# One more pair of gate strips by seven products, and fewer products beside each attention block

## The chip, the cores and the metric

The kernel runs on one core of one Trainium2 chip. The metric is the device time of one execution in microseconds (us); the number that stands for a kernel is the median of its runs. Five engines work side by side: TensorE (PE in the profile) multiplies matrices, VectorE (DVE) and ScalarE (ACT) do element-wise work, GpSimd (POOL) does little here, and SyncE (SP) issues most of the DMAs.

## The reference

One decoder layer on 1024 tokens of width 1024: a SwiGLU half step, a mixer with three branches (an RWKV-7 recurrence, sliding-window attention, cross-attention into 256 memory tokens), and a second SwiGLU half step. What the change touches is the projection into the mixer and the gates that merge the branches:

```python
p_rwkv, p_swa, q_mem, gate_logits = _split(u @ w_in[l], IN_SIZES)
...
g_a, g_b, g_c = _split(jax.nn.sigmoid(gate_logits + gate_b[l]), (D, D, D))
merged = (g_a * (y_a @ w_branch[l, 0]) + g_b * (y_b @ w_branch[l, 1])
          + g_c * (y_c @ w_branch[l, 2]))
```

The gates are 3072 columns of w_in, that is 24 strips of 128 columns, gates 0 to 23.

## The kernel before

**Products.** Everything runs feature-major: a strip of 128 weight columns is multiplied with all 1024 tokens, in two halves of 512. A float32 block is split into a high and a low part (ScalarE casts the high part, line 300, VectorE subtracts it, line 302), and each block product is three matmuls of 128 x 128 on 512 columns (lines 377 to 379). In what follows a *product* is one such matmul; the lumps below are counted in them.

**Two ways to do a strip.** The plain way (`gate_block`, line 1457; in the profile its sums are `pgate`) takes 8 blocks x 2 halves x 3 = 48 products for a strip, 96 for two. The paired way (`win_pair`, line 1407; sums `px`, `py`, `pz`) takes two strips and two halves as a 2 x 2 block matrix and does it with seven half-size products instead of eight: 7 x 4 x 3 = 84. It needs sums of weights, which `operands` (lines 327 to 333) has VectorE make, sums of the inputs (`mix_form`, made once for all pairs), and more steps that put the seven results together (lines 1426 and 1433). Before the change seven pairs are done that way: three of attention strips and gates 2 to 9. The list is `WIN_PAIRS`, line 56.

**The stages of the mixer, in the order of TensorE's stream.** Preparation of the recurrence; two plain gates; the pairs; beside pairs 4 and 5 the corner of a triangular inverse (sums `corner`, small matmuls); the last pair, beside which the first chunks of the recurrence are fetched; the chain of the recurrence (`rwkv_chain`, 16 chunks, each a series of small dependent matmuls `z`, `y`, `gram`, `bkt`), with the plain gates `GATES_FIRST` to `GATES_EARLY` - 1 in its gaps (line 1795); the end of the recurrence; and attention.

**What is beside attention.** `filling` (line 1471) is one long series of products without a place of its own: the plain gates from `GATES_EARLY` to 23, then the first two branch projections (sums `pb`). `fill(n, ...)` takes the next n of them. `attention` (line 1658) has 8 memory blocks and then 8 window blocks. Each block does its scores (`msc` or `sc`), its softmax on VectorE and ScalarE, its transposes (`mptr` or `ptr`) and its values (`mpv` or `pv`), and between these it takes a lump from the series: 42 and 32 products at the first two blocks, then `LUMPS[0]` = 29 at each memory block and `LUMPS[1]` = 52 at each window block. What is left of the series is done behind the last block. Scores, transposes and values share four PSUM banks; a block of window scores needs all four.

**Sums in passing.** `unit` (line 683) is called once behind each plain gate from the start of attention and once behind each strip of the branch projections. Each call makes one of eleven sets of weight sums for the second feed-forward: four VectorE steps (lines 668 to 671) on tiles that SyncE has loaded, and four stores. A set holds two of the four `wide` buffers (line 660; named `gin` in the profile). The other user of these four buffers is the branch projection, which loads a stored gate into one (line 1719, issued by ScalarE's queue), multiplies it with the branch (line 1728) and so frees it.

**What sets the order.** The program is written for a scheduler, which fixes one order for each engine; each engine then works its list from front to end.

Of the kernel before, what the change touches and what calls it, by code (L numbers as in the profile page):

```python
# [47 lines left out]
ATT_BLOCKS = (18, 19, 14, 15, 16, 17, 20, 21, 22, 23)  # L48
GATES_PLAIN = 2
CORNER = (4, 4)  # L50
GATES_FIRST = 10
GATES_EARLY = 12
LUMPS = (29, 52)
MIX_SUMS = ("t2", "t1", "t3", "t4")
PARTS = 5
WIN_PAIRS = ((16, 17), (20, 21), (22, 23)) + tuple((24 + g, 25 + g) for g in range(GATES_PLAIN, GATES_FIRST, 2))

# [174 lines left out]
class Builder:  # L232
# [13 lines left out]
    def plan(self):  # L246
        io, seq = self.io, []
        for f in ("ffn1", "ffn2"):
# [3 lines left out]
            if f == "ffn1":  # L252
# [6 lines left out]
                seq += [("win_pair", i) for i in range(len(WIN_PAIRS))]  # L259
                seq += [("win", 24 + g) for g in range(GATES_FIRST, 24)]  # L260
                seq += [("wb", 4 * i + q) for i in BRANCHES + BRANCHES[2:] for q in range(4)]
# [1209 lines left out]
    def filling(self, u, pool, gate_d, y_d):  # L1471

        for g in range(GATES_EARLY, 22):
            ps = {h: self.psum("pgate") for h in (0, 1)}
# [266 lines left out]
    def mixer(self, u, cp, close_raws, att_d, gate_d, km_d, vm_d):  # L1741
# [22 lines left out]
        with tc.tile_pool(reuse_waits="tile", name="gates", bufs=2) as gp:  # L1764
# [27 lines left out]
            with chunks, tc.tile_pool(reuse_waits="tile", name="chain", bufs=2) as pool:  # L1792
                y = pool.tile([P, NPAIR, T], F32, name="y", bufs=1)
                last = self.rwkv_chain(pool, early, fetched, pk_d, inv_d, y)
                for g in range(GATES_FIRST, GATES_EARLY):
                    self.gate_block(g, u, gp, gate_d)
# [5 lines left out]
            with tc.tile_pool(reuse_waits="tile", name="att", bufs=1) as ap, tc.tile_pool(name="attw", bufs=2) as pool:  # L1802
# [53 lines left out]
                blocks += [WindowBlock(self, pool, b, att_d=att_d, sws=sws, tables=(cos, sin), kd=kd, vt=vt, vd=vd, y_d=y_d[1]) for b in range(nb)]  # L1856
                self.attention(blocks, [42, 32] + [LUMPS[0]] * (nb - 2) + [LUMPS[1]] * nb, {0: [tables], 1: [keys], 2: [load_values], 4: [turn_values]})
                for _ in self.fills:
# [209 lines left out]
```

## Time and profile before

| | us |
|---|---|
| runs of the kernel before, median of 3 | 2256.55 |
| lowest, highest | 2255.4, 2257.11 |
| the profiled execution, its own time | 2257.27 |
| its span, first to last instruction | 2255.6 |
| TensorE busy in it | 2227.7 |
| VectorE busy | 1642.0 |
| ScalarE busy | 1028.9 |

The profiled execution is 0.72 us over the median and its time is 1.67 us more than its span. A busy matmul engine is not one at its peak, since matmuls are pipelined and overlap in the record; how long one takes in a stream is read from the starts of consecutive ones.

### The profile page before, as it was taken

What the parts mean: (1) busy time and instruction counts of PE and PEld (TensorE: products, weight loads), DVE (VectorE), ACT (ScalarE), POOL (GpSimd) and SP (SyncE); (2) the same over time, 40 slices, a digit from 0 to 9 for tenths busy, and PEclk for the clock granted to TensorE, in tenths of its full rate; (3) what the DMA queues carried; (4) which work ended last, traced back from release to release, by engine and by line L of the source; (5) the groups of instructions that cost most, each with busy time, mean ns of one, the idle gap of its engine ahead of it and who ended that gap; (6) DMA issues with size and microseconds to landing.
All of it is one profiled execution on the core that took longest, in us unless ns stands there. A gap on an engine that the chain in (4) does not pass through costs nothing.

```text
span 2255.6 us, 34511 instructions
## 1 busy us (share of the span) xinstructions
PE 2227.7 (99%) x12304; PEld 1832.2 (81%) x12304; DVE 1642.0 (73%) x2761; ACT 1028.9 (46%) x1933; POOL 58.8 (3%) x114
## 2 busy tenths in 40 slices
PE   8999999999999999999999999999999999999998
PEld 6888888888887788877878887788888888888887
DVE  6988767766698887863667577794898886656576
ACT  6523333454556654444355454444663223345451
POOL 0000000000000000000330000000000000000000
PEclk9999999999999999999999999999999999999999
DMA  8565666686665356464538877564565552347663
GB/s 292 174 202 169 202 210 214 229 294 205 191 210 188 120 150 204 155 169 153 158 95 276 270 252 250 185 202 142 174 214 176 194 189 100 114 164 249 205 196 121
DMA packets 279132, 431.90 MB, mean 191 GB/s; under 512 B 58512, under 2 KB 96912, under 8 KB 278704
## 3 DMA queue, kind: packets, MB, share of 16 engines
q1 hardware_dynamic: 266160, 409.96, 56.0%
q10 hardware_dynamic: 12800, 19.73, 2.7%
q8 instruction: 97, 1.59, 0.3%
q14 instruction: 75, 0.61, 0.1%
HBM read 292.75 MB, written 135.79 MB: 190 GB/s over the span
## 4 chain that ended last, share of the span: by engine, by line
PE 51%; DMA 1%; DVE 1%; ACT 1%; issue 0%; SPq 0%; DVEq 0%; ACTq 0%
PE px L377 4%; PE px L379 4%; PE px L378 4%; PE po L377 3%; PE po L378 3%; PE po L379 3%; PE pgate L377 2%; PE pgate L378 2%; PE pgate L379 2%; PE pz L377 2%; PE pz L379 2%; PE pz L378 2%; PE pb L377 2%; PE pb L378 2%; PE pb L379 2%; PE pw L378 1%
## 5 line engine op out<-in xcount | busy, mean ns | idle before, releaser
L300 ACT CAST w_hi<-w_raw 128x512 fp32r<-128x512 f32 x608 | 376.2, 620 | 725.0 <-PE px L378 189.9
L302 DVE TENSOR_TENSOR w_lo<-w_raw,w_hi 128x512 fp32r<-128x512 f32 x608 | 417.3, 688 | 191.0 <-ACT w_hi L300 171.7
L379 PE MATMUL po<-u,w_lo 128*128 128x512 f32 (+1 forms) x476 | 180.9, 380 | 0.0
L378 PE MATMUL po<-u,w_hi 128*128 128x512 f32 (+1 forms) x476 | 180.9, 380 | 0.0
L377 PE MATMUL po<-u,w_hi 128*128 128x512 f32 (+1 forms) x476 | 180.9, 380 | 0.0
L377 PE MATMUL px<-u,w_hi 128*128 128x512 f32 x380 | 147.9, 389 | 0.8 <-DVE km L1596 0.8
L377 PE MATMUL pz<-u,w_hi 128*128 128x512 f32 x380 | 148.1, 390 | 0.0
L378 PE MATMUL px<-u,w_hi 128*128 128x512 f32 x380 | 147.9, 389 | 0.0
L379 PE MATMUL px<-u,w_lo 128*128 128x512 f32 x380 | 147.8, 389 | 0.0
L379 PE MATMUL pz<-u,w_lo 128*128 128x512 f32 x380 | 147.8, 389 | 0.0
L378 PE MATMUL pz<-u,w_hi 128*128 128x512 f32 x380 | 147.8, 389 | 0.0
L377 PE MATMUL px<-f,w_hi 128*128 128x512 f32 x352 | 137.1, 390 | 0.0
L379 PE MATMUL px<-f,w_lo 128*128 128x512 f32 x352 | 137.0, 389 | 0.0
L378 PE MATMUL px<-f,w_hi 128*128 128x512 f32 x352 | 136.9, 389 | 0.0
L486 DVE TENSOR_TENSOR u<-hid,u 128x512 fp32r<-128x512 f32 x114 | 78.3, 690 | 44.7 <-ACT u L485 43.7
L378 PEld LDWEIGHTS po<-u,w_hi 128*128 128x128 f32 x476 | 89.5, 188 | 17.2
L379 PEld LDWEIGHTS po<-u,w_lo 128*128 128x128 f32 x476 | 89.5, 188 | 17.0
L377 PE MATMUL pgate<-u,w_hi 128*128 128x512 f32 x256 | 103.3, 403 | 0.0
L377 PEld LDWEIGHTS po<-u,w_hi 128*128 128x128 f32 x476 | 89.5, 188 | 16.8
L378 PE MATMUL pgate<-u,w_hi 128*128 128x512 f32 x256 | 101.0, 395 | 0.0
L485 ACT CAST u<-hid 128x512 fp32r<-128x512 f32 x114 | 70.6, 620 | 65.0 <-DMA hid<-form_d 54.2
L379 PE MATMUL pgate<-u,w_lo 128*128 128x512 f32 x256 | 100.3, 392 | 0.0
(453 smaller groups left out, 5162.1 us busy)
## 6 DMA issues: line engine op xcount, KB each, us to landing
w_raw<-in_ffn_in SPq DMA_DIRECT2D x224, 256.0 KB
hid<-form_d SPq DMA_DIRECT2D x154, 256.0 KB
w_raw<-in_win SPq DMA_DIRECT2D x112, 256.0 KB
form_d<-g SPq DMA_DIRECT2D x88, 256.0 KB
w_raw<-ffn_sum_d SPq DMA_DIRECT2D x88, 256.0 KB
form_d<-h SPq DMA_DIRECT2D x66, 256.0 KB
w_raw<-in_ffn_out SPq DMA_DIRECT2D x66, 256.0 KB
first_d<-first SPq DMA_DIRECT2D x48, 256.0 KB
```

The costliest lines, as they stand in the source:

```text
L300: self.nc.scalar.copy(hi, x)
L302: self.split_last = self.nc.vector.tensor_tensor(lo, x, hi.bitcast(F32), ALU.subtract)
L377: mm(out, wh, xh, start=first, stop=False, **kw)
L378: mm(out, wh, xl, start=False, stop=False, **kw)
L379: self.last_mm = mm(out, wl, xh, start=False, stop=last, **kw)
L485: self.nc.scalar.copy(hi, x)
L486: self.nc.vector.tensor_tensor(lo, x, hi.bitcast(F32), ALU.subtract)
```

## The change

```diff
 CORNER = (4, 4)
-GATES_FIRST = 10
-GATES_EARLY = 12
-LUMPS = (29, 52)
+GATES_FIRST = 12
+GATES_EARLY = 14
+LUMPS = (24, 46)
 MIX_SUMS = ("t2", "t1", "t3", "t4")
```

Gates 10 and 11 become the eighth pair. The plain gates beside the chain are now 12 and 13, and the series beside attention begins with gate 14: it has 96 products less. The lumps at the six later memory blocks and the eight window blocks are smaller by 6 x 5 + 8 x 6 = 78; the remaining 18 are missing behind the last block. The corner stays beside pairs 4 and 5, and the chunks are fetched beside the new last pair.

TensorE, in the middle of the last pair before the change. `pgate` is the first plain gate of those beside the chain. Before:

```order
L379 MATMUL pz<-mix_form,w_lo 128x512
L377 MATMUL pgate<-u,w_hi 128x512
L378 MATMUL pgate<-u,w_hi 128x512
L377 MATMUL pgate<-u,w_hi 128x512
L377 MATMUL px<-mix_form,w_hi 128x512
```

and at the same place in the stream now (`px<-u` is the first product of the pair after it):

```order
L379 MATMUL pz<-mix_form,w_lo 128x512
L377 MATMUL px<-u,w_hi 128x512
L378 MATMUL px<-u,w_hi 128x512
L377 MATMUL px<-mix_form,w_hi 128x512
L378 MATMUL px<-mix_form,w_hi 128x512
```

In all 11 `pgate` products stood inside the last pair before (3 here, 8 a few rows on); now none does, and the gates beside the chain begin in the chain.

TensorE, the end of the chain. `bkt` ends a chunk's series; `z<-sv,gz` is the first step of the next, which needs the state `sv` that VectorE makes. Before, where the 96 products of the two gates come to an end:

```order
L1250 MATMUL bkt<-ident,f 128x128 x4
L378 MATMUL pgate<-u,w_hi 128x512
L379 MATMUL pgate<-u,w_lo 128x512
L1211 MATMUL z<-sv,gz 64x64 x8
L1211 MATMUL y<-gz,uv 64x64 x8
L1211 MATMUL y<-f,sv 64x64 x8
L1211 MATMUL z<-z,dinv 64x64 x8
L1211 MATMUL y<-center,f 64x64 x8
L1211 MATMUL gram<-f 128x128 x8
L1211 MATMUL z<-uv,bk 64x64 x8
L1250 MATMUL bkt<-ident,f 128x128 x4
L1211 MATMUL z<-sv,gz 64x64 x8
```

and now, at the last `bkt` of the chain:

```order
L1250 MATMUL bkt<-ident,f 128x128 x4
L379 MATMUL pgate<-u,w_lo 128x512
L377 MATMUL pgate<-u,w_hi 128x512
L378 MATMUL pgate<-u,w_hi 128x512
L379 MATMUL pgate<-u,w_lo 128x512
L377 MATMUL pgate<-u,w_hi 128x512
L378 MATMUL pgate<-u,w_hi 128x512
L1211 MATMUL z<-sv,gz 64x64 x8
L1211 MATMUL y<-gz,uv 64x64 x8
L1211 MATMUL y<-f,sv 64x64 x8
L1211 MATMUL z<-z,dinv 64x64 x8
L379 MATMUL pgate<-u,w_lo 128x512
```

Before, two products stand behind the last `bkt` but one and none behind the last; now six stand behind each, as in the chunks ahead of them. Behind the chain 13 products follow where 12 did.

VectorE, beside window blocks, in a branch projection. L668 is the first step of a set of sums, L135 and L139 take scores out of PSUM and find their maximum, L1728 multiplies a branch with its gate, L169 (just behind these rows before) takes transposes out of PSUM. Before, at the last of the sets:

```order
L668 TENSOR_TENSOR gin<-gin 128x512
L140 SCALAR_TENSOR_TENSOR st<-st,sinks 128x8
L1628 TENSOR_TENSOR qs<-qs,cos 128x512
L141 TENSOR_SCALAR st<-st 128x8
L142 TENSOR_TENSOR st<-sinks,st 128x8
L1630 TENSOR_TENSOR qs<-qs,qsw_12028 128x512
L669 TENSOR_TENSOR gin<-gin 128x512
L1728 SCALAR_TENSOR_TENSOR u<-gin,pb 128x512 x2
L302 TENSOR_TENSOR w_lo<-w_raw,w_hi 128x512
L670 TENSOR_TENSOR gin<-gin 128x512
L1629 TENSOR_TENSOR qsw_12029<-qsw_12029,sin 128x512
L671 TENSOR_TENSOR gin<-gin 128x512
```

and now, at the last set but one:

```order
L668 TENSOR_TENSOR gin<-gin 128x512
L135 COPY_PREDICATED sc<-is_before,sc 128x256 x2
L669 TENSOR_TENSOR gin<-gin 128x512
L139 TENSOR_REDUCE st<-sc 128x8
L1628 TENSOR_TENSOR qs<-qs,cos 128x512
L140 SCALAR_TENSOR_TENSOR st<-st,sinks 128x8
L670 TENSOR_TENSOR gin<-gin 128x512
L141 TENSOR_SCALAR st<-st 128x8
L142 TENSOR_TENSOR st<-sinks,st 128x8
L1630 TENSOR_TENSOR qs<-qs,qsw_12173 128x512
L1728 SCALAR_TENSOR_TENSOR u<-gin,pb 128x512
L302 TENSOR_TENSOR w_lo<-w_raw,w_hi 128x512
```

Because gates 10 and 11 no longer call `unit`, two sets move: before, two sets (the tenth and the eleventh) have their L668 behind the start of the first branch projection, now four have (the eighth to the eleventh).

## Rows read from the trace of the kernel before

**Rows 1.** The page: span, and busy us, share and count of each engine.
```profile
span 2255.6 us, 34511 instructions
...
PE 2227.7 (99%) x12304; PEld 1832.2 (81%) x12304; DVE 1642.0 (73%) x2761; ACT 1028.9 (46%) x1933; POOL 58.8 (3%) x114
```

**Rows 2.** Waits of PE, last pair of stages on: us in total, times, longest.
```profile
PE px L377 <- DVE att L1433: 3.4, 1, 3.4
PE z L1211 <- DVE sv L1302: 1.8, 2, 1.1
PE sc L101 <- DVE pt L169: 0.8, 1, 0.8
PE var L1337 <- DVE ysq_lo L1327: 0.8, 1, 0.8
```

**Rows 3.** Windows, two whole pairs: us, busy (instructions) by engine, granted clock, DMA.
```profile
957.17:976.21 19.04, 19.04 (x86) 15.77 (x85) 18.63 (x34) 6.30 (x12) 0.00 (x0) 1.00 0.33 113
976.21:995.25 19.04, 19.04 (x86) 15.77 (x85) 11.94 (x24) 10.43 (x16) 0.00 (x0) 1.00 0.64 232
```

**Rows 4.** Timeline of PE, end of the chain: start us, us, instruction, [idle before].
```profile
1150.97 0.48 PE L378 MATMUL pgate<-u,w_hi 128*128 128x512 f32 x1
...
1152.54 0.69 PE L1211 MATMUL z<-sv,gz 128*64 128x64 f32 x16
...
1157.55 0.48 PE L378 MATMUL pgate<-u,w_hi 128*128 128x512 f32 x1
1157.87 0.40 PE L379 MATMUL pgate<-u,w_lo 128*128 128x512 f32 x1
1159.05 0.69 PE L1211 MATMUL z<-sv,gz 128*64 128x64 f32 x16 [0.79 <-DVE sv L1302]
...
1163.85 0.66 PE L1250 MATMUL bkt<-ident,f 128*128 128x128 f32 x4 [0.17 <-ACT uv L1231]
1165.56 0.69 PE L1211 MATMUL z<-sv,gz 128*64 128x64 f32 x16 [1.05 <-DVE sv L1302]
...
1167.72 0.50 PE L377 MATMUL pgate<-u,w_hi 128*128 128x512 f32 x1
```

**Rows 5.** Windows, attention: memory blocks, first window blocks, the other window blocks.
```profile
1209.00:1333.00 124.00, 124.00 (x670) 106.19 (x669) 78.81 (x161) 58.85 (x149) 1.96 (x3) 1.00 0.83 271
1333.00:1389.00 56.00, 56.00 (x294) 43.68 (x294) 43.54 (x102) 27.79 (x92) 0.00 (x0) 1.00 0.86 289
1389.00:1460.00 71.00, 70.16 (x374) 54.32 (x373) 52.44 (x122) 33.71 (x113) 0.00 (x0) 1.00 0.55 177
```

**Rows 6.** Waits of VectorE beside the window blocks.
```profile
DVE gin L668 <- DMA gin<-in_ffn_out: 7.0, 3, 3.5
```

**Rows 7.** Timeline of VectorE beside one window block.
```profile
1383.74 0.69 DVE L668 TENSOR_TENSOR gin<-gin 128x512 f32<-128x512 f32 x1 [3.50 <-DMA gin<-in_ffn_out]
...
1386.77 1.27 DVE L1728 SCALAR_TENSOR_TENSOR u<-gin,pb 128x512 f32<-128x512 f32 x2
...
1390.37 1.28 DVE L169 TENSOR_TENSOR pt<-ptr,is_own 128x512 f32<-128x512 f32 x2
```

**Rows 8.** Timeline of SyncE: issue of the last load that this VectorE step waits for.
```profile
1375.89 0.42 SPq L654 DMA_DIRECT2D gin<-in_ffn_out  x1
```

**Rows 9.** Timeline of ScalarE beside the same block (ACTq issues a DMA).
```profile
1388.08 0.33 ACTq L1719 DMA_DIRECT2D gin<-gate_d  x1
1388.50 0.59 ACT L1685 COPY yo<-pv 128x512 f32<-128x512 f32 x1 [5.54 <-PE pb L378]
```

**Rows 10.** Timeline of PE at the same block.
```profile
1382.07 1.09 PE L104 MATMUL ptr<-ident,sc 128*128 128x128 f32 x8
...
1388.56 1.71 PE L101 MATMUL sc<-kd,qs 64*128 64x256 f32 x8
1391.11 1.73 PE L101 MATMUL sc<-kd,qs 64*128 64x256 f32 x8 [0.84 <-DVE pt L169]
1392.77 0.50 PE L377 MATMUL pb<-u,w_hi 128*128 128x512 f32 x1
```

**Rows 11.** Timeline of PE at the block after it.
```profile
1408.22 2.10 PE L101 MATMUL sc<-kd,qs 64*128 64x256 f32 x16
1410.25 0.50 PE L377 MATMUL pb<-u,w_hi 128*128 128x512 f32 x1
```


## The prediction

> **What bounds the kernel now.** I read the page first, then the waits of PE, then the stages that the change touches. PE is busy for 2227.7 of the span's 2255.6 us, VectorE 73% and ScalarE 46% [rows 1]. The waits of PE from the last plain gates before the pairs to the end of attention are few: 3.4 us beside the corner, 1.8 in two pieces in the chain, 0.8 at a window block's scores, 0.8 at the end of the chain [rows 2]. So the kernel's time is PE's stream, one product after another, and a change to it is worth the products it takes out, plus the idle spots it fills, less the spots it opens.
>
> A product's price is read from a pair: 84 products in 19.04 us, with no idle time, at the granted clock of 1.00 (the higher level, 2.4 GHz; the row's count of 86 has the neighbours that reach over its edges) [rows 3]. That is 0.2267 us each. In such a window VectorE is busy 11.9 us where nothing else runs beside the pair, 18.6 where the inverse does [rows 3].
>
> **The change part by part.**
>
> *Twelve products less.* Gates 10 and 11 take 84 products instead of 96: 12 x 0.2267 = **-2.72 us**. The new pair runs behind the corner and ahead of the last pair, where no inverse is left, so its weight sums, splits and merges have the cover of the second window: 11.9 us of VectorE's work and 10.4 of ScalarE's in 19.04 [rows 3]. I cost them at nothing; if that cover were gone, VectorE's own 11.9 us would be the pair's time, still less than 19. The 3.4 us beside the corner stay, since nothing up to the last pair moves.
>
> The Trainium skill's page "TensorE: Matmul & The Clock Gate", section "Back-to-back issue gap", says that in a stream of weight load and matmul 512 columns take some 131 ns each. The window shows 227, so the measurement decides; by the page's figure the twelve products would be an estimated 1.57 us.
>
> *Eleven products move from the last pair into the chain's end.* This is in the order and not in the table of constants. Before, 11 gate products ran inside the last pair, where PE has no gap; the gates' 96 products then ran out two chunks early, and PE stood idle 0.79 and 1.05 us for the state that VectorE makes [rows 4]. Now six products stand in each of those two spots. The pair loses 11 x 0.2267 = 2.49 us. The tail, from the last `bkt` but one to the products behind the chain, took 1157.55 to 1167.72, 10.17 us with two products in it [rows 4]. With six and six it is: a full chunk as the one ahead, 1150.97 to 1157.55, 6.58; then six products more, 1150.97 to 1152.54, 1.57; then the last steps, 1165.56 to 1167.72, 2.16; together 10.31 [rows 4]. One more product behind it is 0.23. So 10.31 + 0.23 - 10.17 = 0.37 is paid and 2.49 saved: **-2.12 us**. The bounds: six products last 1.57 us and the bare waits were 1157.55 to 1159.05, 1.50, and less at the other spot, so they cover it barely [rows 4]; if the state came as much later, the 0.79 + 1.05 = 1.84 us of idle would be there again, and -2.12 + 1.84 = -0.3 would be left. A gain over 2.49 is excluded, since that is all that the pair gives up.
>
> *Smaller lumps beside attention.* That removes 96 products from the series; they are the ones already counted, since gates 10 and 11 left it. What is new is less cover for each block. Memory blocks: PE shows no wait in that stretch, busy for 124.00 of 124 us [rows 5], and each step has a lump of its own and most of another block between it and what needs it. I take zero. Window blocks: one stall in the trace. At 1388.56 the scores took until 1392.77, 4.21 us [rows 10], where the next block's took 1408.22 to 1410.25, 2.03 [rows 11]: 2.18 us lost, of which 0.84 is idle that the profile puts down to L169. The chain behind it: the last load of a set of sums was issued at 1375.89 [rows 8], VectorE stood 3.50 us at the set's first step until 1383.74, and did the merge L1728 at 1386.77 and L169, which empties the transposes' banks, only at 1390.37 [rows 7]. ScalarE waited too: the gate load at 1388.08 needs the buffer that L1728 frees, and the copies of values and transposes stand behind it [rows 9]; the transposes had been ready since 1383 [rows 10]. The DMA engines were busy 0.86 in that stretch and 0.55 after the last set [rows 5].
>
> Now four sets instead of two lie beside branch products. Of the two of before one stalled PE. From below, none does and the 2.18 us go. From above, all four do at that price: 4 x 2.18 - 2.18 = +6.54. In the order two of the four look like the one that stalled (scores or transposes to empty stand behind a set's first step); the eighth has its tiles earlier, and the loads of the ninth are queued ahead of most of a block. I take between one stall, as now, and two: **+1.1 us**, nearest to the one row that there is.
>
> *Sum.* -2.72 - 2.12 + 1.1 = -3.74 us. Against the profiled execution's own 2257.27 that is 2253.5; that one lies 0.72 over the median, so against the median of 2256.55 it is **2252.8 us**, 0.17% less.
>
> **The rivals.**
>
> *Attention gives nothing back.* The sets' loads land in time with the DMA queue spread over more blocks, or the stall of now goes. For it: PE waits little anywhere, and of three sets that kept VectorE waiting beside window blocks, 7.0 us in all [rows 6], one alone reached PE. Against it: less cover at each block. -4.84 gives 2251.7; with the 2.18 gone as well, -7.02, 2249.5.
>
> *The sets hold up VectorE and PE waits for it.* Four sets beside branch products, each holding two of four buffers, each with its first step ahead of work that empties PSUM. Decisive from 2.18 + 4.84 = 7.0 us of stalls in all, 1.76 for each of the four; then it is slower than before. At 2.18 each: 2256.55 - 4.84 + 6.54 = 2258.3; at VectorE's longest wait, 3.5 each [rows 6], 14.0 - 2.18 = 11.8 more, 2263.5. For it: rows 7, 9 and 10 are that chain once, and there are 46 products instead of 52 to hide it. Against it: two sets did not stall. The Trainium skill's page "PSUM — Partial Sum Buffer", section "Engine vs sequencer instructions", says that ScalarE's and VectorE's queues are strictly first in, first out, which speaks against a change that puts more waiting steps in them; the trace agrees, with ready transposes left from 1383 to 1389 [rows 9, 10].
>
> *The chain does not take the moved products for nothing.* The six products are pushed apart by the gates' weight splits, or the state comes late: -2.72 - 0.3 + 1.1 = -1.9, 2254.6.
>
> **How the numbers follow.** A measurement of this kernel can tell about 0.2%, 4.5 us, from no change, so the line lies at 2252.0. The forecast, both gains and one to two stalls, 0.50. Attention gives nothing back, 0.33. The sets hold up PE, 0.08, of which half is over 2261.1. The chain takes no more for nothing, 0.09. The forecast's own spread reaches a little over the line at 2252.0, the second case a little under it. Faster by over 0.2%: 0.35; within: 0.61; slower: 0.04. The range leaves out the lower part of the second case and most of the third: 2250.2 to 2256.6.
>
> **What would show it.** In the changed kernel's profile: eight pairs of 19.04 us, with no wait of PE in the new one; no gate products in the last pair; no wait of PE for the state at the chain's last two chunks, and the chain's tail some 10.3 us; the wait beside the corner still 3.4; beside window blocks four sets of sums among the branch products, and between one and two places where scores or transposes take some 2 us more than at the other blocks. The prediction is wrong if the new pair or the last one waits for VectorE, if memory blocks begin to show waits at their transposes (their banks are then the limit), or if PE's waits beside window blocks sum to over 5 us.

## The result and the profile after

The changed kernel takes 2265.35 us (median of 6 runs, 2263.3 to 2267.47); the kernel before, on the same chip, 2256.83 (6 runs). The ratio is 1.0040, with a 95% interval of 1.0029 to 1.0051: 0.4% slower, 8.5 us.

The page's head shows TensorE's idle time grown: the span rose by 9.9 us and PE's busy time by 1.9 (it counts more us for fewer instructions, since some ran at a lower clock), where [rows 1] had 2227.7 of 2255.6.

```profile
span 2265.5 us, 34524 instructions
...
PE 2229.6 (98%) x12292; PEld 1832.2 (81%) x12292; DVE 1646.6 (73%) x2771; ACT 1034.0 (46%) x1939; POOL 59.2 (3%) x114
```

Waits of PE over the whole execution (us in total, times, longest) answer [rows 2]: the corner's 3.4 us is unchanged, the chain's waits for `sv` are gone, and beside the window blocks 6.5 us and 3.4 us stand where 0.8 stood.

```profile
PE sc L101 <- DVE pt L169: 6.5, 2, 5.1
...
PE pv L101 <- DVE sc L135: 3.4, 1, 3.4
PE px L377 <- DVE att L1433: 3.4, 1, 3.4
```

Windows of 19.04 us over the last two pairs, the added one being among the eight (us, busy us and instructions by engine, granted clock, DMA share, GB/s), answer [rows 3]: PE has no gap in either.

```profile
1041.28:1060.32 19.04, 19.04 (x85) 15.77 (x84) 8.51 (x13) 7.52 (x13) 0.00 (x0) 1.00 0.62 166
1060.32:1079.36 19.04, 19.04 (x85) 15.77 (x84) 7.45 (x12) 9.21 (x16) 1.91 (x4) 1.00 0.71 229
```

Timeline of PE at the end of the chain, answering [rows 4] (start, us, instruction; an idle time before it stands in brackets): six products stand behind each of the last two `bkt`, and no `z<-sv,gz` waits. From 1175.53 to the products behind the chain at 1186.03 it is 10.50 us.

```profile
1175.53 0.48 PE L379 MATMUL pgate<-u,w_lo 128*128 128x512 f32 x1
...
1177.10 0.69 PE L1211 MATMUL z<-sv,gz 128*64 128x64 f32 x16
...
1181.88 0.66 PE L1250 MATMUL bkt<-ident,f 128*128 128x128 f32 x4 [0.16 <-ACT uv L1231]
1182.30 0.48 PE L379 MATMUL pgate<-u,w_lo 128*128 128x512 f32 x1
...
1183.87 0.69 PE L1211 MATMUL z<-sv,gz 128*64 128x64 f32 x16
...
1186.03 0.50 PE L379 MATMUL pgate<-u,w_lo 128*128 128x512 f32 x1
```

Windows over attention, cut as in [rows 5]: the memory blocks are full, 124.00 of 124 us; the window blocks are not, and the granted clock there is 0.96.

```profile
1209.00:1333.00 124.00, 124.00 (x652) 106.02 (x651) 85.06 (x160) 59.99 (x138) 1.96 (x3) 1.00 0.82 271
1333.00:1389.00 56.00, 50.80 (x271) 39.82 (x270) 39.87 (x99) 27.59 (x99) 0.00 (x0) 0.96 0.83 274
1389.00:1460.00 71.00, 66.21 (x348) 49.99 (x347) 57.11 (x139) 33.40 (x113) 0.00 (x0) 0.96 0.63 204
```

Up to the first memory block's scores the new order costs what the first two terms of the sum say, and all that went wrong lies beside the window blocks. How much that is can be read from one stretch, from the first window block's scores to the last one's values. In the kernel before:

```profile
1311.62:1459.14 147.52, 146.68 (x797) 115.63 (x796) 111.56 (x262) 70.06 (x231) 0.00 (x0) 1.00 0.70 227
```

and in the changed kernel:

```profile
1323.99:1473.39 149.40, 139.41 (x746) 108.21 (x745) 112.63 (x265) 68.80 (x228) 0.00 (x0) 0.97 0.69 222
```

Counted by the starts of matmuls it is 796 matmuls in 147.53 us before and 745 in 149.40 after. The 51 fewer are products, 51 x 0.2267 = 11.56 us; the stretch should have taken 135.97 and took **13.4 us more**. With the two other terms, -2.72 - 2.12 + 13.4 = +8.6. To compare this with the profiled executions, take the time from the first product of the pairs to the first one behind the branch projections (`pw`). Before:

```profile
916.37 0.39 PE L377 MATMUL px<-u,w_hi 128*128 128x512 f32 x1
...
1520.52 0.39 PE L377 MATMUL pw<-u,w_hi 128*128 128x512 f32 x1
```

and now:

```profile
917.85 0.39 PE L377 MATMUL px<-u,w_hi 128*128 128x512 f32 x1
...
1530.69 0.39 PE L377 MATMUL pw<-u,w_hi 128*128 128x512 f32 x1
```

That is 604.15 and 612.84 us, +8.7. The span rose by 9.9, since this execution was already 1.5 us later where the pairs start, ahead of anything that the change touches; the medians differ by 8.5.

**One stall, step by step.** The largest of the stalls is at a block's scores. Timeline of PE:

```profile
1380.92 1.14 PE L101 MATMUL sc<-kd,qs 64*128 64x256 f32 x8
1387.16 2.67 PE L101 MATMUL sc<-kd,qs 64*128 64x256 f32 x8 [5.10 <-DVE pt L169]
1389.76 0.79 PE L377 MATMUL pb<-u,w_hi 128*128 128x512 f32 x1
```

The scores took 1380.92 to 1389.76, 8.84 us, where a block without a stall takes 2.03 [rows 11]; 5.10 us of it is idle, for L169, which empties the transposes' banks. Timeline of VectorE:

```profile
1373.31 1.22 DVE L139 TENSOR_REDUCE st<-sc 128x8 f32<-128x1024 f32 x1
1380.78 0.69 DVE L1628 TENSOR_TENSOR qs<-qs,cos 128x512 f32<-128x512 f32 x1 [6.25 <-DMA qs<-att_d]
1381.39 0.16 DVE L140 SCALAR_TENSOR_TENSOR st<-st,sinks 128x8 f32<-128x8 f32 x1
1381.46 0.69 DVE L668 TENSOR_TENSOR gin<-gin 128x512 f32<-128x512 f32 x1
...
1386.42 1.28 DVE L169 TENSOR_TENSOR pt<-ptr,is_own 128x512 f32<-128x512 f32 x2
```

VectorE finished the score maximum L139 at 1374.53 and then stood 6.25 us at L1628, the rotation of a *later* block's queries, for their load. Behind it stood L140 to L142 (the softmax that ScalarE's exponentials wait for), a set of sums (L668 on), two merges, and L169 at 1386.42. Timeline of SyncE:

```profile
1362.70 2.86 SPq L673 DMA_DIRECT2D ffn_sum_d<-gin  x4
...
1368.55 1.29 SPq L654 DMA_DIRECT2D gin<-in_ffn_out  x3
...
1371.44 0.33 SPq L654 DMA_DIRECT2D gin<-in_ffn_out  x1
1371.88 0.38 SPq L113 DMA_DIRECT2D qs<-att_d  x1
```

SyncE sent that query load at 1371.88, behind four loads of the next set and, before these, the four stores of the last one. VectorE could start 8.90 us after the load was sent.

The Trainium skill's page "DMA: Bandwidth & Descriptors", section "Queues, rings and completion order", says that on each DMA engine the descriptors of one queue are consumed in order, while queues take turns. The trace does not show the order on one DMA engine. What it shows: the three query loads that VectorE waited for in this kernel took 4.5, 8.9 and 6.4 us from issue to use; the three that it waited for in the run without the late sets (e_no_late_sets, below) took 4.0, 5.9 and 5.6; and with a queue of their own (e_q_pool) the loads took a median of 4.8 us from issue to landing. So two of the three were slower here than any of the three without the late sets, and one was not.

Waits of VectorE in that stretch show the same for all blocks. The first steps of sets, which [rows 6] had at 7.0 us and the prediction made its reason, are the lesser part:

```profile
DVE qs L1628 <- DMA qs<-att_d: 9.8, 3, 6.2
DVE pt L169 <- ACT pt L166: 6.1, 3, 4.4
DVE gin L668 <- DMA gin<-in_ffn_out: 3.2, 1, 3.2
```

### The profile page after: what moved, and what is told of

Same layout as the page of the kernel before. It is cut to its first block, busy times and chain, and to the rows that moved or that the text cites. A ratio compares the mean times of both kernels' runs of the same rounds, so it can differ in the third digit from the quotient of the medians.

```text
span 2265.5 us, 34524 instructions
## 1 busy us (share of the span) xinstructions
PE 2229.6 (98%) x12292; PEld 1832.2 (81%) x12292; DVE 1646.6 (73%) x2771; ACT 1034.0 (46%) x1939; POOL 59.2 (3%) x114
## 4 chain that ended last, share of the span: by engine, by line
PE 49%; DVE 2%; DMA 2%; issue 1%; ACT 1%; SPq 0%; ACTq 0%; DVEq 0%
PE px L377 4%; PE px L379 4%; PE px L378 4%; PE po L378 3%; PE po L377 3%; PE po L379 3%; PE pz L377 2%; PE pz L378 2%; PE pz L379 2%; PE pgate L379 2%; PE pgate L377 2%; PE pgate L378 2%; PE pw L377 1%; PE pw L378 1%; PE pw L379 1%; PE pb L377 1%
## 5 line engine op out<-in xcount | busy, mean ns | idle before, releaser
L377 PE MATMUL pgate<-u,w_hi 128*128 128x512 f32 x224 | 90.4, 403 | 0.0
L379 PE MATMUL pgate<-u,w_lo 128*128 128x512 f32 x224 | 89.2, 398 | 0.0
L377 PE MATMUL pr<-u,w_hi 128*128 128x512 f32 x224 | 87.5, 392 | 0.0
```

The source lines that it names most:

```text
L377: mm(out, wh, xh, start=first, stop=False, **kw)
L379: self.last_mm = mm(out, wl, xh, start=False, stop=last, **kw)
```

## The experiments

Theory A, after this reading: the sets of sums that now lie beside branch products make the stalls. Theory B: the smaller lumps do, 46 products being too little cover. The table gives all runs; *surplus* is the stretch of the window blocks in the profiled execution, over before's 147.53 us less 0.2267 for each product fewer. *Memory* is what the memory blocks took, from their first scores to the first window block's, over 86.04 us (the changed kernel's), where that is over 0.5. A dash: other products lie there, not comparable. The ratio is to the kernel before on the same chip.

| kernel | median us | ratio, 95% | surplus | memory |
|---|---|---|---|---|
| the change | 2265.35 | 1.0029 to 1.0051 | 13.4 | |
| e_lumps_old | 2271.93 | 1.0052 to 1.0082 | 8.2 | - |
| e_lumps_only | 2259.53 | 0.9999 to 1.0017 | 2.4 | - |
| e_before_shift | 2257.36 | 0.9994 to 1.0012 | 1.9 | - |
| e_units_back | 2273.01 | 1.0059 to 1.0094 | 11.2 | 9.0 |
| e_no_late_sets | 2253.45 | 0.9974 to 0.9993 | -0.8 | 0.7 |
| e_late_loads_only | 2256.60 | 0.9992 to 1.0011 | 2.9 | |
| e_late_dma_only | 2262.51 | 1.0019 to 1.0043 | 8.4 | |
| e_late_dve_only | 2257.33 | 0.9995 to 1.0014 | 2.4 | |
| e_q_early | 2268.06 | 1.0031 to 1.0065 | 14.9 | |
| e_q_pool | 2262.26 | 1.0015 to 1.0037 | 5.9 | 1.7 |
| e_sets_all_pool | 2262.95 | 1.0012 to 1.0036 | 6.8 | 4.3 |
| e_gin_pool | 2263.77 | 1.0020 to 1.0041 | 8.9 | |
| e_both_pool | 2266.91 | 1.0032 to 1.0062 | 11.2 | 1.8 |
| e_wide5 | 2264.54 | 1.0019 to 1.0045 | 10.6 | |
| e_wide2_later5 | 2255.72 | 0.9986 to 1.0005 | 2.9 | 1.2 |
| e_sets_later3 | 2258.79 | 1.0002 to 1.0021 | 5.1 | |
| e_sets_later5 | 2253.20 | 0.9978 to 0.9997 | -0.4 | |
| e_before_sets_later | 2255.35 | 0.9989 to 1.0007 | -2.4 | - |

Runs of a kernel with stalls spread by up to 9 us (the change itself by 4.2), so a surplus of one profiled execution can be 3 us off its median; where they differ, the median decides. The kernel before had a median of 2256.28 to 2256.83 on the chips of these runs, so medians of two rows compare to about 0.6 us, beside the spread of each.

### Is it the lumps, or the place of the branch strips?

**e_lumps_old**, the change with the lumps of before:

```diff
-LUMPS = (24, 46)
+LUMPS = (29, 52)
```

> The changed kernel with the lumps of before (29 and 52 products beside a block); the eighth pair and the two fewer plain gate strips stay, so the sets of sums and the branch strips still come earlier among the blocks. Theory A (what the blocks' in-order engines wait for: the query loads of the window blocks, which SyncE sends behind the sets' buffer-bound loads, makes the stalls, whatever the size of the lumps): the waits of TensorE beside window blocks stay at 8 to 16 us, time 2258 to 2267. Theory B (the smaller cover makes them): waits of TensorE there at most 3 us, time 2252 to 2254 (2256.8 - 4.84 for the pair and the chain's end).

2271.93 us, slower than the change. Stalls stayed (surplus 8.2, 5.2 less than the change's, so the cover may have a part in them), and more came behind the last block, where the series had run out too early and PE waited 5.6 us for the inputs of the third branch:

```profile
PE pb L377 <- ACT y L485: 5.6, 2, 4.8
PE sc L101 <- DVE pt L169: 3.0, 3, 1.4
```

**e_lumps_only**, the kernel before with the lumps of the change:

```diff
-LUMPS = (29, 52)
+LUMPS = (24, 46)
```

> The kernel before with only the lumps of the change (24 and 46); pairs and plain gate strips as before. Theory A (the moved sets and branch strips make the stalls): waits of TensorE beside window blocks stay within 5 us, time 2256 to 2260. Theory B (the smaller cover makes them): waits of some 15 us as in the changed kernel, time 2268 to 2271 (2256.8 + 13.3), with nothing gained by an eighth pair.

2259.53 us; the interval reaches from no change to 0.17% slower. PE has one wait beside the blocks:

```profile
PE ptr L104 <- DVE sc L157: 1.4, 1, 1.4
```

**e_before_shift**, the kernel before with the same number of products beside the blocks, but the branch strips half a strip earlier among the window blocks:

```diff
-LUMPS = (29, 52)
+LUMPS = (33, 49)
```

> The kernel before with lumps of 33 and 49 products instead of 29 and 52: as many in all, but the branch strips start some 24 products (half a strip) earlier among the window blocks, as in the change; seven pairs as before. Rival E (the place of the branch strips among the blocks decides): TensorE's waits beside window blocks rise from 0.8 us to 7 us or more, time 2263 to 2270. Theory D, by the number of sets beside branch strips (three as before): at most 4 us, time 2255 to 2260.

2257.36 us, no difference. (By time, two sets of the kernel before start behind its first branch product, not the three that the expectation says; here too.) These three together: larger lumps don't cure the change, smaller lumps alone cost 0 to 4 us, and an earlier start of the branch strips alone costs nothing that can be measured. Theory B falls as the main cause, as does the rival E that the expectations name.

### Is it the sets?

**e_no_late_sets**, without the last five of the eleven sets (loads, VectorE steps and stores; the second feed-forward block reads other sets' sums in their place):

```diff
-        for q in range(KP):
+        for q in range(6):
...
-        return self.sum_d[f][SUMS.index(a), q] if a in SUMS else self.io[f + "_out"][a, q]
+        return self.sum_d[f][SUMS.index(a), q - 6 if f == "ffn2" and q > 5 else q] if a in SUMS else self.io[f + "_out"][a, q]
```

> The changed kernel without the last five of the eleven sets of sums, those that are made beside branch products: their loads, VectorE operations and stores are left out, and the second feed-forward block reads the first five sets' sums in their place. Theory D (the sets and the gate loads of the branch strips share four wide buffers; a load that waits for one stands at the head of an in-order queue, SyncE's with the query loads behind it, ScalarE's with the exponentials and score copies behind it): TensorE's waits beside window blocks fall from about 14 us over before to at most 3 us, time 2251 to 2254. Rival E (the place of the branch strips among the blocks, and VectorE's own order, whatever the sets do): waits stay at 7 us or more, time 2259 to 2266.

2253.45 us: 11.9 less than the change, and the surplus is gone. Without these five sets one wait of PE is left beside the window blocks, 1.4 us at values. Theory A holds this far.

**e_units_back**, two of the sets moved to the plain gates:

```diff
             self.gate_out(g, ps, pool, gate_d)
             self.unit()
+            if g in (16, 19):
+                self.unit()
```

> The changed kernel, but two of the plain gate strips beside the memory blocks make a second set each, so that as many sets as before the change lie beside gate products and two fewer beside the branch products of the window blocks. Theory A in its form that the two added sets make the stalls: waits of TensorE beside window blocks at most 4 us, nothing new beside memory blocks, time 2252 to 2255. Theory B (smaller cover alone) or the branch strips' own loads: waits stay at 10 us or more, time 2262 to 2267.

2273.01 us, the slowest of all: a miss for theory A as it stood. The memory blocks, which had never stalled, took 9.0 us more: PE waited 3.2 us for the load of the values and 2.7 for the first window block's queries. And the window blocks, with three sets beside branch products, still lost 11.2, 5.6 of it at one merge. So it isn't the *number* of sets beside branch products alone: the kernel before has two of them there and loses 2.2 us. Waits of PE beside attention in that run:

```profile
PE pb L377 <- DVE u L1730: 6.6, 3, 5.6
PE vtr L1850 <- DMA v_in<-att_d: 3.2, 1, 3.2
PE sc L101 <- DVE qs L1632: 2.7, 1, 2.7
```

### Which part of a set?

**e_late_dma_only**, the last five sets without their VectorE steps, with loads and stores:

```diff
         with self.tc.issue_after(behind.ins):
+          if f == "ffn1" or q < 6:
             V.tensor_tensor(a22, a21, a22, ALU.add)
...
```

> The changed kernel without the VectorE operations (L668 to L671) of the last five sets of sums; their loads and stores stay, so that what is stored are the loaded strips. Leaving out all of the five gave 2253.45. Theory F (VectorE is what the five sets hold up: 2.9 us of operations each, in order, and each first one waits for its load with the blocks' operations behind it): the stalls go, TensorE's waits beside window blocks at most 3 us, time 2251 to 2255. Rival G (the transfers hold up the query loads, gate loads and branch loads, on the queues or in the DMA engines): waits stay at 7 us or more, time 2259 to 2266.

2262.51: 9.1 us over the run without the sets. The transfers are the larger part (rival G), against theory F.

**e_late_dve_only**, their VectorE steps without transfers:

```diff
-            for n, t in enumerate(a):
+            for n, t in enumerate(a if f == "ffn1" or q < 6 else ()):
...
+        if f == "ffn2" and q > 5:
+            x, y = (t[:, :TH].rearrange("p (k c) -> p k c", c=P) for t in self.cos_sin)
+            with self.tc.issue_after(behind.ins):
+                for t in (a22, a21, a11, a12):
+                    V.tensor_tensor(t, x, y, ALU.add)
+            return
...
```

> The changed kernel without the loads and stores of the last five sets; their VectorE operations stay, on the two rotation tables that lie in SBUF, so that they never wait for a load (the sums that the second feed-forward block reads are other sets'). Theory F in the form that the 2.9 us of operations themselves are too many: 2260 to 2266, as the change. Theory F in the form that VectorE's wait for the loads is what costs, or rival G: 2251 to 2255.

2257.33: 3.9 us over the run without the sets. Both parts cost, 3.9 + 9.1 = 13.0 against 11.9 together.

**e_late_loads_only**, the loads alone:

```diff
...
+        if f == "ffn2" and q > 5:
+            return
         a11, a12, a21, a22 = a
```

> The changed kernel with the loads of the last five sets, but without their VectorE operations and stores (the second feed-forward block reads other sets' sums). Without all of it 2253.45, with loads and stores 2262.51. If the stores, which wait on SyncE's queue for the loads to land and hold up what is behind them, make most of the 9 us: 2253 to 2257. If the loads do, by the buffers that they take from the gate loads: 2258 to 2263.

2256.60: 3.2 us. So the stores add 5.9 more, with all that SyncE's waits for them bring (a store waits for its load to land, and a buffer is held until it is stored). In the run with loads and stores SyncE stood at stores (L674 there) until what they store had landed, and VectorE waited for query loads and for their swapped rows. Waits of SyncE beside the window blocks of the run with loads and stores:

```profile
SPq L674 <- DMA gin<-in_ffn_out: 7.3, 6, 2.4
...
SPq L1636 <- DMA gin<-in_ffn_out: 3.8, 2, 2.2
```

and of VectorE in the same run:

```profile
DVE qs L1629 <- DMA qs<-att_d: 10.5, 4, 4.7
...
DVE qsw L1630 <- DMA qsw<-att_d: 5.0, 2, 2.8
```

### Is it SyncE's queue, ScalarE's, or the buffers?

**e_q_early**, the query loads asked for as early as the memory blocks' are:

```diff
-        nc.sync.dma_start(self.qs, src)
         sw = self.sws[self.b % 2]
-        self.k.load_swapped(sw, src)
+        with self.k.tc.high_priority(offset=self.k.lead):
+            nc.sync.dma_start(self.qs, src)
+            self.k.load_swapped(sw, src)
```

> The changed kernel, with the query loads of the window blocks (the load and the four loads of the swapped rows) asked for as early as those of the memory blocks are, so that SyncE sends them ahead of the sets' loads. Theory A in its form that the late query load (L1628 waited 9.8 us) is the cause: VectorE's waits for query loads fall under 3 us, TensorE's waits beside window blocks fall to 4 to 7 us (the third stall, on a score copy of ScalarE, is not touched), time 2255 to 2259. Theory B: TensorE's waits stay at 13 us or more, time 2262 to 2267.

2268.06, no gain. The edit did only half of what it was meant to: the query loads beside branch products were still sent no more than 5.4 to 8.2 us before their use, behind stores and loads of sets, and VectorE's waits for them fell from 9.8 us to 4.8, not under 3. TensorE stood 5.6 us for the step that empties the transposes' banks (L169 in the change) at one block and 5.3 for a merge at another. VectorE's waits at gate loads (6.4 us) and at ScalarE's exponentials (6.1) are its longest there. A miss: halving the wait for query loads gave nothing back, so the late query load is how one stall of the change came about, and what all depends on is not shown to be that.

**e_q_pool**, the query loads on GpSimd's queue, which is empty there:

```diff
-        nc.sync.dma_start(self.qs, src)
+        nc.gpsimd.dma_start(self.qs, src)
         sw = self.sws[self.b % 2]
-        self.k.load_swapped(sw, src)
+        self.k.load_swapped(sw, src, nc.gpsimd)
...
```

> The changed kernel with the query loads of the window blocks (the load and the four loads of the swapped rows) issued by GpSimd, whose queue holds nothing else there, instead of SyncE. If the place behind the sets' transfers on SyncE's queue is what makes the query loads late, and the late query loads are what the transfers cost: VectorE's waits for query loads (9.8 us in the change) fall under 3 us, time 2255 to 2259. If the transfers themselves are slow, or the stalls come by another way: 2261 to 2267.

2262.26: 3.1 us less than the change. VectorE's waits for the queries themselves fall to 0.2 us beside the window blocks, but those for the swapped rows, which the same edit moves, rise to 8.0 us in three, so the block's own loads still hold it up:

```profile
DVE qsw L1629 <- DMA qsw<-att_d: 8.0, 3, 4.5
```

The 3.1 us is thus what this move gave back, not all that late query loads cost. DMA issues of that run (count, KB each, median us from issue to landing):

```profile
qs<-att_d POOLq DMA_DIRECT2D x6, 256.0 KB, 4.8
```

**e_sets_all_pool**, all loads and stores of the sets on GpSimd's queue:

```diff
-                self.nc.sync.dma_start(t, self.io[f + "_out"][n, q])
+                (self.nc.gpsimd if f == "ffn2" else self.nc.sync).dma_start(t, self.io[f + "_out"][n, q])
...
-            nc.sync.dma_start(self.sum_d[f][SUMS.index(n), q], t)
+            (nc.gpsimd if f == "ffn2" else nc.sync).dma_start(self.sum_d[f][SUMS.index(n), q], t)
```

> The changed kernel with all loads and stores of the eleven sets issued by GpSimd, so that SyncE's queue has none of them; gate loads stay with ScalarE, and the four wide buffers and the traffic are as they were. Queue of SyncE as the cause: 2255 to 2259. Traffic or shared buffers as the cause: 2261 to 2267, VectorE waiting for query loads or gate loads as before.

2262.95: 2.4 us less. The window blocks lost 6.8 us instead of 13.4, and the memory blocks, where sets now came at other times, lost 4.3. Together with the run before it: taking transfers off SyncE's queue gave back 2 to 3 us by the medians, and in neither run the whole. (In the window blocks alone the surplus fell by 7.5 and 6.6 us in these two profiles; a part of that was lost again beside the memory blocks.)

**e_gin_pool**, the gate loads of the first two branches on GpSimd's queue, so that ScalarE never stands at one:

```diff
-            nc.scalar.dma_start(g, gate_d[i * KD + o][:, cols])
+            (nc.scalar if i == BRANCHES[2] else nc.gpsimd).dma_start(g, gate_d[i * KD + o][:, cols])
```

> The changed kernel with the gate loads of the first two branches (L1719) issued by GpSimd, which has no other work beside these blocks, instead of ScalarE. Theory D: ScalarE no longer stands before a gate load that waits for a buffer, so its share of the stalls goes (the third, 3.4 us and what follows it, and part of the first), the query loads behind SyncE's set loads stay late: time 2257 to 2262, TensorE's waits beside window blocks 4 to 9 us. Rival E: 2263 to 2267.

2263.77: 1.6 us less than the change, and inside the spread of both.

**e_both_pool**, the same with the sets' loads on GpSimd's queue too (their stores stay with SyncE):

```diff
-                self.nc.sync.dma_start(t, self.io[f + "_out"][n, q])
+                (self.nc.gpsimd if f == "ffn2" else self.nc.sync).dma_start(t, self.io[f + "_out"][n, q])
```

> As the run before it, and the sets' loads (L654, 11 sets of four) issued by GpSimd too, so that nothing that waits for a wide buffer stands ahead of the query loads on SyncE or of ScalarE's work. Theory D: TensorE's waits beside window blocks at most 4 us, time 2251 to 2256. Rival E: 2262 to 2267. Should a load that GpSimd issues cost the other engines something, the memory blocks would show it too, where before and the change have no wait at all.

2266.91, no gain. Theory D, that loads waiting for a buffer at the head of a queue are all of it, falls with this run and the next two.

**e_wide5**, a fifth `wide` buffer:

```diff
-        return self.widepool.tile([P, T], F32, tag="wide", name="gin", bufs=4)
+        return self.widepool.tile([P, T], F32, tag="wide", name="gin", bufs=5)
...
-        yin = lambda: self.yin.tile([P, TH], F32, tag="yin", name="yin", bufs=4)
+        yin = lambda: self.yin.tile([P, TH], F32, tag="yin", name="yin", bufs=3)
...
-        n = pool.tile([P, T], F32, name="turns", bufs=1)
+        n = cos
...
-                        sw = p2.tile([P, T], F32, name="k_sw")
+                        sw = vt.rearrange("p b c -> p (b c)")
...
```

> The changed kernel with a fifth wide buffer, for which the rotation tables' scratch lies in the cosine table, the swapped keys lie in the value tile, and the branch inputs have three buffers instead of four. If buffers held by the sets are the larger part of the 9 us of transfers: 2256 to 2261, with TensorE's waits beside window blocks 3 to 8 us lower. If traffic or queues are: 2262 to 2267.

2264.54, within the spread of the change. **e_wide2_later5**, two `wide` buffers in the run of 2253.20 below:

```diff
-        return self.widepool.tile([P, T], F32, tag="wide", name="gin", bufs=4)
+        return self.widepool.tile([P, T], F32, tag="wide", name="gin", bufs=2)
...
```

> The run of 2253.2 (last five sets beside the second feed-forward block's pairs) with two wide buffers instead of four, as many as a set leaves to the gate loads of the branch strips while it holds its own two. If the buffers that a set holds until its stores have landed are what its transfers cost: time 2257 to 2264, with TensorE's waits beside window blocks back to 5 us or more and ScalarE's queue standing at gate loads (the memory blocks, whose six sets then have no second pair of buffers, may lose some time too, to be counted apart). If buffers don't matter: 2252 to 2255.

2255.72: 2.5 us more than with four, of which 1.2 lie beside the memory blocks. So buffers are at most a small part of what the transfers cost. (The fifth buffer was paid for with one of the branch inputs' four, so its run alone would not exclude them.)

### Can the pair be had without the stalls?

**e_sets_later5**, the change with the last five sets made beside the second feed-forward block's pairs, as the first block's sets are beside its own:

```diff
-                if f == "ffn1" and FIRST[f] <= j < FIRST[f] + KP:
-                    self.sums_made(f, j - FIRST[f], self.sums_loads(f, j - FIRST[f], self.sums_tiles(pool)), made)
+                q = j - FIRST[f] + (6 if f == "ffn2" else 0)
+                if j >= FIRST[f] and q < KP:
+                    self.sums_made(f, q, self.sums_loads(f, q, self.sums_tiles(pool)), made)
...
-        for q in range(KP):
+        for q in range(6):
```

> The changed kernel with the same work, but the last five sets are made beside the last pairs of the second feed-forward block's first layer, as those of the first block are, instead of beside branch products. If the five sets beside branch products are the whole of the stalls, and the pairs take them at no cost as they do in the first block: 2251 to 2255, faster than the kernel before (2256.8 - 4.84 plus some tenths). If the pairs have no room for them: 2256 to 2262, with new waits in the second feed-forward block.

2253.20 us, ratio 0.9987 (0.9978 to 0.9997): faster than the kernel before by 0.13%, and 12 us less than the change with the same work. Its window blocks take 135.58 us where 135.97 were worked out above:

```profile
1323.36:1458.94 135.58, 133.75 (x746) 105.31 (x746) 102.13 (x247) 68.63 (x228) 0.00 (x0) 1.00 0.52 166
```

PE has one wait beside attention, at values, as the 3.4 us of the change were, so a part of those needs no late set:

```profile
PE pv L101 <- DVE sc L135: 1.8, 1, 1.8
```

From the first product of the pairs to the first one behind the branch projections it takes 599.18 us, 4.97 less than the kernel before, where the first two terms of the sum make 4.84:

```profile
917.05 0.39 PE L377 MATMUL px<-u,w_hi 128*128 128x512 f32 x1
...
1516.23 0.39 PE L377 MATMUL pw<-u,w_hi 128*128 128x512 f32 x1
```

The pairs of the second feed-forward block take the sets for nothing: from that `pw` to the end of the execution it is 735.0 us with them and 735.0 before. A window there, with VectorE at 63 us of 85 and PE without a gap:

```profile
1890.00:1975.00 85.00, 85.00 (x376) 70.38 (x375) 63.05 (x103) 31.51 (x54) 0.00 (x0) 1.00 0.62 207
```

**e_sets_later3**, only the last three moved (`range(8)`, and 8 for 6 above):

```diff
-        for q in range(KP):
+        for q in range(8):
```

> As the run before it, but only the last three sets are moved; two stay beside branch products, as many as the kernel before makes there after its first branch product. If each set costs alike (12 us by five, 2.4 each): 2256 to 2259. If the stalls set in only with the third set: 2251 to 2255.

2258.79: two sets left beside the start of the branch strips cost 5.6 us, the three others 6.6. So in the changed kernel the five cost some 2.4 us each on average (12.15 / 5).

**e_before_sets_later**, the kernel before with its last three sets moved the same way (`range(8)`), a control:

> The kernel before (seven pairs, lumps of 29 and 52) with its last three sets made beside the last pairs of the second feed-forward block, as in the run of 2253.2, so a control of it: what moving sets gives without the eighth pair. If before has next to no stalls to lose (PE waited 0.8 us): 2255.5 to 2257.5. If sets beside branch products cost 2.4 us each there as well: 2249 to 2252.

2255.35, no measurable difference to before (0.9989 to 1.0007), though PE's one wait beside the window blocks is gone in its profile. So of the 3.3 us of e_sets_later5 some 2.3 remain for the eighth pair, by medians (2256.53 - 2253.20 less 2256.40 - 2255.35).

## Why the prediction was wrong

Predicted 2252.8 us, range 2250.2 to 2256.6, with 0.04 for slower. Measured 2265.35.

- *What bounds the kernel*: right. All of the difference is PE's stream: products out, idle spots in.
- *Twelve products less, -2.72*: right; eight pairs without a wait in the added one, the corner's 3.4 us unchanged.
- *Eleven products moved into the chain's end, -2.12*: right. No waits for the state; the tail was 10.50 us for the 10.31 worked out. e_sets_later5, where both of these terms stand alone, is 3.3 us under before by its medians (interval 0.5 to 5.0), against 4.84 by the sum; in its profile the stretch that the change touches is 4.97 shorter, so the two terms together are right there, and the rest lies outside it.
- *Smaller lumps beside attention, +1.1*: **the step that failed.** It measured +13.4, twice its upper bound of +6.54. Three things were wrong in it. First, the bound was the price of the one stall in the trace times the number of sets; but the stalls have no common price: over the time of a block without a stall the changed kernel lost 0.9, 6.8 and 2.2 us at three blocks' scores and 4.8 around one block's values, where before lost 2.18 once. (That the stall of before was small because its block still had slack is an argument, not shown.) Second, it looked only at a set's own first step, L668, in VectorE's order. A set also puts eight transfers of 256 KB on the queues that the blocks' own loads use, and for the five sets these cost more (9.1 us) than the VectorE steps (3.9). The trace of before had a row of it, among VectorE's waits beside window blocks, which the prediction passed over:

```profile
DVE qs L1628 <- DMA qs<-att_d: 2.1, 3, 1.6
```

  In the changed kernel this row is 9.8 us. Third, in the list of what lies there, the four sets named (here and with the change) were one too few by time: the seventh set's first step, at 1351.99, ran behind the first branch product, at 1350.76.
- *The number of lumps' products as the cover*: right as far as it went: smaller lumps alone cost 0 to 4 us (e_lumps_only), not the 13.4.
- *The rival "The sets hold up VectorE and PE waits for it"*, at 0.08, is what happened, from a higher price: 2263.5 was its end, 2265.35 the time. "Attention gives nothing back" is near what e_sets_later5 shows, but only with five sets moved away. The chances were the wrong way round: the argument against the rival, that two sets did not stall, did not carry over to five.
- *What would show it*: the sign that was named, PE's waits beside window blocks summing to over 5 us, is what the profile shows (6.5 + 3.4).

What is shown: the stalls need the last five sets beside the branch products, by leaving them out and by moving them; of their cost the transfers are two thirds to three quarters, and the larger part of that comes only with the stores; smaller lumps, the branch strips' place, the gate loads on ScalarE's queue and the number of buffers, each changed alone, account for 4 us or less. What stays open: how the transfers do it. Two moves off SyncE's queue gave back 2 to 3 us of 9 by the medians, each with new waits beside it, so the full share of that queue is open. That the rest comes from a block's loads of all kinds landing later, each a few us and on whichever engine has least slack, fits the traces (where VectorE waited less for query loads, PE's waits were for other steps, as in e_q_early), but each edit also made the scheduler choose another order, and no run took the traffic away and left the order as it was.

## What to carry to other kernels

Side work that fits beside one kind of product need not fit beside another: count what it adds to every in-order queue it shares (its loads and its stores, not only its arithmetic), and ask what stands behind each. Where a stall in the trace is to be multiplied, don't take its price as the upper end: here four stalls lay between 0.9 and 6.8 us, where the one of before was 2.18. When a step that saves time takes away the cover of side work, look first for another stage to put that work in; here that turned 0.4% slower into 0.13% faster.

## What the runs showed of the hardware

The idle spot costs more than its length. After the 5.10 us in which PE stood at the scores (1382.06 to 1387.16 above), the granted clock was 0.50, the lower of its two levels (1.2 GHz), in the window in which work resumed, and 0.95 in the next:

```profile
1376.00:1381.00 5.00, 5.00 (x24) 3.85 (x23) 0.22 (x1) 0.25 (x1) 0.00 (x0) 1.00 0.59 210
1381.00:1386.00 5.00, 1.06 (x8) 0.63 (x8) 5.00 (x12) 3.29 (x17) 0.00 (x0) 0.87 0.43 149
1386.00:1391.00 5.00, 3.84 (x11) 2.81 (x12) 4.93 (x16) 0.00 (x0) 0.00 (x0) 0.50 0.99 317
1391.00:1396.00 5.00, 5.00 (x22) 4.00 (x21) 4.31 (x9) 1.72 (x5) 0.00 (x0) 0.95 0.87 273
```

Those scores took 6.81 us over their 2.03, and the 24 products behind them 6.49 us, where 24 behind another block's scores in this run (from 1407.50 to 1413.17) took 5.67: 7.6 us for 5.1 of idle. In the stretch of the window blocks PE's waits sum to 9.9 us and the surplus is 13.4.
